# Whole-row modulation products in the opening, a longer landing time in the planner, and the spatial-gate constants in another buffer

## The chip, the cores and the metric

The kernel runs on one core of a Trainium2 chip. TensorE (PE) multiplies matrices, VectorE (DVE), ScalarE (ACT) and GpSimd (POOL) work element by element, and SyncE (SP) issues the DMAs, all of them through one queue in order. Each engine works through its own list of instructions in order, and waits at an instruction until the data and the buffers that it needs are there. The metric is the device time of one execution in microseconds; lower is better.

## The reference

Two layers of a trunk with three branches each (grouped attention, gated linear attention "GLA", and a spatial-gating unit "SGU"), over 512 latent and 256 context tokens with 1024 channels, all in float32. Cut to what matters:

```python
shift, scale, gate = split(silu(c) @ w_ada + b_ada, 3)          # 1024 x 3072
h = x * (1 + scale) + shift                                     # and hc from ctx with c_ctx
a_q, a_k, ..., s_u, s_v, s_g, m_a, m_g, m_s = split(h @ w_in)   # 1024 x 7456
y_attn = attention(a_q, a_k, a_v) * silu(a_g)
y_gla = gla(g_q, g_k, g_v, ...) * silu(g_g)
mixed = w_s @ layer_norm(s_v, ln_g, ln_b) + b_s                 # per group and 128-token chunk
y_sgu = s_u * mixed * silu(s_g)
m = sigmoid(m_a) * (y_attn @ w_br_attn) + sigmoid(m_g) * (y_gla @ w_br_gla) + sigmoid(m_s) * (y_sgu @ w_br_sgu)
x = layer_norm(alpha * x + gate * (m @ w_out), post_g, post_b)
```

## The kernel before

Every large product is made of three matmuls of split operands: a float32 array is split into a rounded high part (ACT, `hi`, `hlh`, `wh`, `yh`) and the rest (DVE, `lo`, `hll`, `wl`, `yl`; line 575, shown as L128), and high x high, high x low and low x high are summed in PSUM (`mm3`, line 625). Weights come in pieces of 256 channels x 256 columns (`raw`, three buffers).

*The planner.* Nothing runs in the order in which it is written. Each instruction is recorded, and `Sched.order` (line 138) plays the whole program through with a cost for each instruction and a latency between engines, takes the ready instruction of the best priority on each engine, and does this in 16 rounds with new priorities; the best round's order is what each engine gets (line 387). A DMA is reckoned in line 325: at the earliest 1300 ns after its issue, its bytes at 335 per ns, and then 700 ns until it has landed (line 328). That reckoned landing does not delay anything on the chip; it decides where in its engine's list an instruction that uses the data is put.

*The opening* (`start0`, line 1457). The first layer's shift and scale are dot products of rows of `w_ada` with silu(c) and silu(c_ctx). For each of eight channel blocks kb, `load` (line 1477) brings 128 rows of 1024 for the shift and 128 for the scale, and `dots` (line 1491) multiplies them with the broadcast row `srow` on DVE, in halves of 512 with a sum each: four instructions for c (v = 0, out to `junk`) and four for c_ctx (v = 1, in place in `wada`), then two small additions into `svec`. Then ACT applies `svec` to the inputs `xs`, both halves of the split are made (`hlh`/`hll` for the latent, `hch`/`hcl` for the context tokens), and PE adds this block's part of the first projection (`mmt`, line 1467). The blocks kb = 0, 1, 4 and 5 have one tile of 2 x 1024 each (tags T4 and T5), the others four tiles of 512.

*The second layer's middle.* `sgc` (line 1226) holds the four constants of the SGU: two layer-norm rows, the bias and the 128 x 512 weights. It lies in the single buffer T3, in which before it lies `yat`, the attention output, and after it `mac0`, the sum over the branches. `kept` tiles (tag S3, eight buffers) are gate values that were put to DRAM earlier and are read back: those of `sud` and `sgd` are multiplied onto the SGU's `ymix` (lines 1245 to 1249), those of `md` get a sigmoid (line 1265) and are multiplied with the first branch's products into `mac` (line 1280, `branch`). In the same stretch the dot products of the later gates run on DVE (`ada_dot`, line 676).

Of the kernel before, what the change touches and what calls it, by code (L numbers as in the profile page):

```python
# [13 lines left out]
ALU = mybir.AluOpType  # L14
# [8 lines left out]
C_GQ, C_GK, C_GV, C_GG = 1280, 1536, 1792, 2336  # L23
C_SU, C_SV, C_SG = 2848, 3360, 3872
C_MA, C_MG, C_MS = 4384, 5408, 6432


class Sched:
# [109 lines left out]
    def order(self, prio):  # L138
# [31 lines left out]
        dma, cur, ticks, acted = 0.0, None, {}, 0.0  # L170
# [10 lines left out]
        def freed(x, e):  # L181
            return x[0] + (self.lag(gone[x[1]], e) if x[1] >= 0 else 0.0)
# [33 lines left out]
        while done < n:  # L216
            best = None
            for e in engs:
# [7 lines left out]
                t = free[e] if R else (L[0][0] if L else None)  # L226
# [7 lines left out]
            t, e = best  # L234
# [25 lines left out]
            elif e in held and R and held[other[e]] > t + 1.0:  # L260

                w = held[other[e]] - t
# [25 lines left out]
            w = max((freed(x, e) for k_, c in need.items() for x in heapq.nsmallest(c, tagat[k_])), default=0.0)  # L288
# [36 lines left out]
            if e == "SP":  # L325
                dma = max(dma, st + 1300.0) + cost
                free[e] = max(st + 60.0, dma - self.AHEAD)
                end = dma + 700.0
            else:
                end = free[e] = st + cost  # L330
                if e == "ACT":
                    acted = end
                if e in held and e in self.port[i]:
                    held[e] = end
# [170 lines left out]
def kernel(ctx: ExitStack, tc: tile.TileContext, A, out, dbg=None):  # L505
    nc = tc.nc
    sc = Sched(nc)
    ACT, DVE, POOL, PE, SP = sc.ACT, sc.DVE, sc.POOL, sc.PE, sc.SP
# [8 lines left out]
    def T(tag, shape, dt=F32, name=None):  # L517
        return sc.tile(sb, shape, dt, tag, BUFS.get(tag, 1), name or tag, "SB")

    def PS(tag, shape, dt=F32):  # L520
        return sc.tile(psp, shape, dt, tag, 2, tag, "PS")
# [4 lines left out]
    def C(shape, dt=F32, name=None):  # L526
        return sc.tile(const, shape, dt, "c_" + name, 1, name, "SB")
# [5 lines left out]
    def act(out, in_, func=AF.Copy, **kw):  # L533
        return ACT.activation(out=out, in_=in_, func=func, **kw)

    def tt(eng, out, in0, in1, op):
        return eng.tensor_tensor(out=out, in0=in0, in1=in1, op=op)
# [24 lines left out]
    bcols = [pk[:, 0:24], pk[:, 24:48]]  # L562
# [10 lines left out]
    def split(hi, lo, src):  # L573
        act(hi, src)
        tta(lo, src, f(hi), ALU.subtract)
# [49 lines left out]
    def mm3(ps, L, R, first, last):  # L625

        PE.matmul(ps, L[0], R[0], start=first, stop=False)
        PE.matmul(ps, L[0], R[1], start=False, stop=False)
        PE.matmul(ps, L[1], R[0], start=False, stop=last)
# [72 lines left out]
    svecs = [C([128, 2, 8, 2], F32, name=f"svec{l}") for l in range(2)]  # L702
# [8 lines left out]
    def layer(l, X, start=None):  # L711
        full = l == 0
# [325 lines left out]
        for pr in range(2):  # L1038
# [49 lines left out]
            for gi in range(2):  # L1088
# [4 lines left out]
                for lvs in LEVELS:  # L1093
                    ps = PS("s", [128, 2, 512])
                    calls, kq, views, off, cost = [], [], {}, 0, SWITCH_PE
                    for lv in lvs:
# [23 lines left out]
                        w = 64 if lv in (1, 7) else 32  # L1120
# [21 lines left out]
                    for lv in lvs:  # L1142
                        v = views[lv]
# [69 lines left out]
        sv = T("T5", [128, 6, 512], name="sv")  # L1213
# [9 lines left out]

        lab(f"{l}sgu")

        sgc = T("T3", [128, 4, 512], name="sgc")
        lg, lb, bs, wsT = (sgc[:, i] for i in range(4))
        SP.dma_start(out=lg, in_=A["sgu_ln_g"][l].partition_broadcast(128))
        SP.dma_start(out=lb, in_=A["sgu_ln_b"][l].partition_broadcast(128))
# [56 lines left out]
        srow = ada_rows(nv)  # L1286
# [170 lines left out]
    def start0():  # L1457
        srow = ada_rows(2, "p")
        sA, sB, sC = PS("s", [128, 1024]), PS("s", [128, 1024]), PS("pt", [128, 512])
        acc = {2: (sA[:, 0:512], sA[:, 512:768]), 3: (sB[:, 0:512], sB[:, 512:768]),  # L1460
               4: (PS("p", [128, 512]), sA[:, 768:1024]), 5: (PS("p", [128, 512]), sB[:, 768:1024]),
               0: (PS("pt", [128, 512]), sC[:, 0:256]), 1: (None, sC[:, 256:512])}
        Wh = [T(t_, [128, 4, 768], F32R, name="wh") for t_ in ("T0", "T1")]
        Wl = [T(t_, [128, 4, 768], F32R, name="wl") for t_ in ("T2", "T3")]
        W = [(Wh[k // 4][:, k % 4], Wl[k // 4][:, k % 4]) for k in range(8)]

        def mmt(t, k, o, ps, joint=False):

            seg, off = ("c", t * 128) if t < 2 else ("l", (t - 2) * 128)
            H = (X0[seg][0][:, k, off:off + 128], X0[seg][1][:, k, off:off + 128])  # L1470
            n = ps.shape[-1]
            mm3(ps, H, (W[k][0][:, o:o + n], W[k][1][:, o:o + n]), k == 0 and not joint, k == 7 and not joint)

        junk = T("Q2", [128, 512], name="junk")
        part = {}

        def load(kb):
            tags = ("T4", "T5", ("hi", "hi", "lo", "lo"), ("hi", "hi", "lo", "lo"))[kb % 4]
            if kb % 4 < 2:
                t = T(tags, [128, 2, 1024], name="wada")  # L1480
                w = [t[:, j // 2, 512 * (j % 2):512 * (j % 2) + 512] for j in range(4)]
                for j in range(2):
                    SP.dma_start(out=t[:, j], in_=A["w_adaT"][0, 8 * j + kb])
            else:
                w = []
                for j in range(4):
                    w.append(T(tags[j], [128, 512], name="wada"))
                    SP.dma_start(out=w[j], in_=A["w_adaT"][0, 8 * (j // 2) + kb, :, 512 * (j % 2):512 * (j % 2) + 512])
            part[kb] = w, T("aa", [128, 2, 2, 2])

        def dots(kb, v, npool):

            w, ac = part[kb]
            for j in (0, 2, 1, 3):
                row = srow[:, v, 512 * (j % 2):512 * (j % 2) + 512]
                a = ac[:, v, j // 2, j % 2:j % 2 + 1]
                if npool == 1 and j == 3 or npool == 2 and j > 1 or npool == 3 and j:
                    o = w[j] if v else T("Q2", [128, 512], name="prod")
                    tt(POOL, o, w[j], row, ALU.mult)
                    act(o, o, accum_out=a)  # L1500
                else:
                    DVE.scalar_tensor_tensor(out=w[j] if v else junk, in0=w[j], scalar=1.0, in1=row,
                                             op0=ALU.mult, op1=ALU.mult, accum_out=a)
            if kb == 0 and v == 0:
                for b_ in bcols:
                    ts(DVE, b_[:, 8:16], b_[:, 8:16], 1.0, ALU.add)
            sv = svecs[0][:, :, kb, v]
            tt(DVE, sv, ac[:, v, :, 0], ac[:, v, :, 1], ALU.add)
            tt(DVE, sv, sv, bcols[0][:, kb:16:8], ALU.add)

        def modulate(seg, si, kb, v):
            sh, scl = (svecs[0][:, w, kb, si:si + 1] for w in range(2))
            sc.alt((ACT, "activation", dict(out=v, in_=v, func=AF.Identity, scale=scl, bias=sh)),
                   (DVE, "tensor_scalar", dict(out=v, in0=v, scalar1=scl, scalar2=sh, op0=ALU.mult, op1=ALU.add)))
            split(X0[seg][0][:, kb], X0[seg][1][:, kb], v)

        zero = T("Q2", [128, 128], F32R, name="zero")
        ts(DVE, zero, ident, 0.0, ALU.mult)

        def bank(first):  # L1520
            for s in (sA[:, 512:1024], sB[:, 512:1024], sC):
                PE.matmul(s, zero, identr.unsqueeze(1).to_broadcast([128, 4, 128]), start=first, stop=not first)

        bank(True)
        for kb in range(AH):
            load(kb)
            dots(kb, 0, NP0)
        for kb in range(8):
            if kb + AH < 8:
                load(kb + AH)  # L1530
                dots(kb + AH, 0, 0)
            xs = T("F3", [128, NT], name="xs")
            SP.dma_start(out=xs[:, sl("l")], in_=A["xT"][:, kb])
            SP.dma_start(out=xs[:, sl("c")], in_=A["ctxT"][:, kb])
            raw = T("S3", [128, 768], name="raw0")
            SP.dma_start(out=raw, in_=A["w_in"][0, kb * 128:kb * 128 + 128, 0:768])
            split(W[kb][0], W[kb][1], raw)
            modulate("l", 0, kb, xs[:, sl("l")])
            dots(kb, 1, NPOOL[kb % 2])
            modulate("c", 1, kb, xs[:, sl("c")])  # L1540
            for t in (2, 3, 4, 5, 0, 1):
                if acc[t][0] is not None:
                    mmt(t, kb, 0, acc[t][0])
                mmt(t, kb, 512, acc[t][1], True)
        bank(False)
        sc.floor = len(sc.ops)

        def st_b(q, ev_kv):
            for t in (2, 3, 4, 5, 0, 1):
                if acc[t][0] is not None:  # L1550
                    act(q[:, t], acc[t][0].rearrange("p (h d) -> p h d", h=8))
                ev_kv(acc[t][1], t)
            ps = PS("p", [128, 512])
            for k in range(8):
                mmt(1, k, 0, ps)
            act(q[:, 1], ps.rearrange("p (h d) -> p h d", h=8))

        return st_b
# [78 lines left out]
```

## Time and profile before

| | us |
|---|---|
| median of 3 runs (lowest, highest) | 1430.35 (1429.0, 1435.49) |
| profiled execution, its own time | 1431.16 |
| its span in the trace | 1429.3 |
| PE busy in the span | 1387.9 |
| DVE, ACT, POOL busy | 1032.5, 671.3, 164.5 |

The profiled execution took 1.86 us more than its span. PE is busy for 97% of it, so what can be lost or won on the chain that ends last is mostly PE's idle time (about 41 us), and the time in which PE works at a lower clock. A row of the trace gives the start and the duration in us, the engine and the line of the recording helper (L421 or L128 for nearly all), the operation with output <- inputs by their program names, and in square brackets how long the engine sat idle before it and what ended that.

### The profile page before, as it was taken

What the parts mean: (1) busy time and instruction counts of PE and PEld (TensorE: products, weight loads), DVE (VectorE), ACT (ScalarE), POOL (GpSimd) and SP (SyncE); (2) the same over time, 40 slices, a digit from 0 to 9 for tenths busy, and PEclk for the clock granted to TensorE, in tenths of its full rate; (3) what the DMA queues carried; (4) which work ended last, traced back from release to release, by engine and by line L of the source; (5) the groups of instructions that cost most, each with busy time, mean ns of one, the idle gap of its engine ahead of it and who ended that gap; (6) DMA issues with size and microseconds to landing.
All of it is one profiled execution on the core that took longest, in us unless ns stands there. A gap on an engine that the chain in (4) does not pass through costs nothing.

```text
span 1429.3 us, 27382 instructions
## 1 busy us (share of the span) xinstructions
PE 1387.9 (97%) x10724; PEld 1227.5 (86%) x10724; DVE 1032.5 (72%) x2206; ACT 671.3 (47%) x1293; POOL 164.5 (12%) x261
## 2 busy tenths in 40 slices
PE   8999999999999999999999999999999998999997
PEld 5798899987888888888889999998987877888887
DVE  8968877897977678732147684897799876645396
ACT  4566667844464323212232174666774554422331
POOL 0021100034330000000000020110014320000003
PEclk9999999999999999999999999999999999999999
DMA  9410012332356765521224232112243467535542
GB/s 321 160 45 9 23 31 65 124 94 64 93 177 207 250 200 169 158 67 45 65 77 148 66 119 71 30 31 60 82 148 90 117 193 252 168 97 177 182 144 94
DMA packets 123956, 168.55 MB, mean 118 GB/s; under 512 B 9497, under 2 KB 90801, under 8 KB 123825
## 3 DMA queue, kind: packets, MB, share of 16 engines
q1 hardware_dynamic: 123826, 166.79, 37.4%
q8 instruction: 84, 1.38, 0.4%
q14 instruction: 46, 0.38, 0.1%
HBM read 143.41 MB, written 23.34 MB: 117 GB/s over the span
## 4 chain that ended last, share of the span: by engine, by line
PE 73%; DVE 16%; DMA 5%; issue 2%; ACT 2%; POOL 1%; SPq 0%; POOLq 0%; DVEq 0%; ACTq 0%
PE p L421 60%; PE pt L421 8%; PE s L421 4%; DVE M L128 3%; DVE lo L128 2%; DMA wada<-in_w_adaT_dram 2%; DVE wada L421 1%; DVE sm L421 1%; DVE junk L421 1%; DMA raw<-in_w_in_dram 1%; PE s L119 1%; DVE PTs L421 1%; DMA sgc<-in_sgu_b_dram 1%; DVE cs L421 1%; POOL sf L421 0%
## 5 line engine op out<-in xcount | busy, mean ns | idle before, releaser
L128 DVE TENSOR_TENSOR lo<-raw,hi 128x512 fp32r<-128x512 f32 (+1 forms) x293 | 202.4, 700 | 173.7 <-ACT hi L421 166.2
L421 ACT ACTIVATE hi<-raw 128x512 fp32r<-128x512 f32 (+1 forms) x296 | 185.8, 634 | 233.2 <-PE p L421 149.8
L421 PE MATMUL p<-hlh,hi 128*128 128x512 f32 x704 | 280.9, 399 | 2.5 <-DVE mac L421 1.5
L421 PE MATMUL p<-hlh,lo 128*128 128x512 f32 x704 | 280.7, 399 | 1.5 <-DVE lo L128 1.3
L421 PE MATMUL p<-hll,hi 128*128 128x512 f32 x704 | 278.6, 396 | 0.0
L421 PEld LDWEIGHTS p<-hlh,lo 128*128 128x128 f32 x704 | 132.4, 188 | 31.6 <-DVE lo L128 2.1
L421 PEld LDWEIGHTS p<-hlh,hi 128*128 128x128 f32 x704 | 132.3, 188 | 29.8 <-ACT hi L421 2.2
L421 PEld LDWEIGHTS p<-hll,hi 128*128 128x128 f32 x704 | 132.3, 188 | 26.5
L421 PE MATMUL p<-hch,lo 128*128 128x256 f32 x368 | 104.5, 284 | 0.0
L421 PE MATMUL p<-hch,hi 128*128 128x256 f32 x368 | 104.2, 283 | 0.0
L421 PE MATMUL p<-hcl,hi 128*128 128x256 f32 x368 | 104.0, 283 | 0.0
L421 PE MATMUL p<-hi,hlh 128*128 128x256 f32 (+1 forms) x352 | 102.0, 290 | 0.0
L421 PE MATMUL p<-hi,hll 128*128 128x256 f32 (+1 forms) x352 | 100.8, 286 | 0.0
L421 PE MATMUL p<-lo,hlh 128*128 128x256 f32 (+1 forms) x352 | 99.8, 284 | 0.0
L421 POOL TENSOR_SCALAR sf<-sf 128x1 f32<-128x1 f32 x20 | 7.5, 374 | 642.3 <-DVE sf L421 641.9
L421 PE MATMUL p<-yh,hi 128*128 128x512 f32 (+1 forms) x192 | 70.0, 364 | 7.8 <-DVE mac L421 6.7
L421 ACT ACTIVATE P<-s,sm 128x768 f32<-128x768 f32 (+1 forms) x80 | 65.4, 821 | 23.5 <-DVE sm L421 23.2
L421 DVE TENSOR_REDUCE sm<-s 128x1 f32<-128x768 f32 (+1 forms) x72 | 65.0, 921 | 12.4 <-PE s L421 12.2
L421 DVE TENSOR_TENSOR PTs<-pt,PTs 128x512 fp32r<-128x512 f32 x104 | 69.2, 685 | 4.1 <-ACT PTs L421 3.1
L421 PEld LDWEIGHTS p<-hcl,hi 128*128 128x128 f32 x368 | 69.3, 188 | 2.1
L421 PEld LDWEIGHTS p<-hch,hi 128*128 128x128 f32 x368 | 69.5, 189 | 1.9
L421 DVE SCALAR_TENSOR_TENSOR wada<-wada,srow 128x512 f32<-128x512 f32 x96 | 65.1, 687 | 8.0 <-DMA wada<-in_w_adaT_dram 6.7
(299 smaller groups left out, 3352.1 us busy)
## 6 DMA issues: line engine op xcount, KB each, us to landing
raw<-in_w_in_dram SPq DMA_DIRECT2D x204, 256.0 KB, 3.0
wada<-in_w_adaT_dram SPq DMA_DIRECT2D x80, 256.0 KB, 4.9
raw<-in_w_out_dram SPq DMA_DIRECT2D x32, 256.0 KB, 2.9
raw<-in_w_in_dram SPq DMA_DIRECT2D x16, 272.0 KB, 3.1
wada<-in_w_adaT_dram SPq DMA_DIRECT2D x8, 512.0 KB, 4.9
raw<-in_w_br_attn_dram SPq DMA_DIRECT2D x16, 256.0 KB, 3.4
raw<-in_w_br_gla_dram SPq DMA_DIRECT2D x16, 256.0 KB, 3.0
raw<-in_w_br_sgu_dram SPq DMA_DIRECT2D x16, 256.0 KB, 3.3
```

The costliest lines, as they stand in the source:

```text
L119: return self.record(eng.n, lambda: [getattr(eng.e, m)(*a, **k) for m, a, k in calls], outs, ins, cost, None, dens)
L128: fns[p.n] = lambda real=real, k=k: real(**k)
L421: return s.record(n, lambda: real(*a, **k), outs, ins, _cost(n, meth, outs, ins, k), _table(n, k), _dens(n, ins, k), _port(n, meth, outs, ...
```

## The change

Three things are changed. The 700 ns of reckoned landing become 2000. In the second layer (`full` is false there) `sgc` takes a buffer of the tag `hc`, in which the context half of the split input lies until its last projection. And for the blocks kb = 1, 4 and 5 the tile has a third row of 1024, and `dots` multiplies whole rows: two instructions of 1024 per v with one sum each, out to the third row for v = 0, and one small addition instead of two.

```diff
+LAND = 2000.0
...
                 dma = max(dma, st + 1300.0) + cost
                 free[e] = max(st + 60.0, dma - self.AHEAD)
-                end = dma + 700.0
+                end = dma + LAND
...
-        sgc = T("T3", [128, 4, 512], name="sgc")
+        sgc = T("T3" if full else "hc", [128, 4, 512], name="sgc")
...
-                t = T(tags, [128, 2, 1024], name="wada")
-                w = [t[:, j // 2, 512 * (j % 2):512 * (j % 2) + 512] for j in range(4)]
+                t = T(tags, [128, 3, 1024], name="wada")
+                w = [t[:, 0], t[:, 1], t[:, 2]] if kb else [t[:, j // 2, 512 * (j % 2):512 * (j % 2) + 512] for j in range(4)]
...
             w, ac = part[kb]
+            sv = svecs[0][:, :, kb, v]
+            if kb % 4 < 2 and kb:
+                for j in range(2):
+                    DVE.scalar_tensor_tensor(out=w[j] if v else w[2], in0=w[j], scalar=1.0, in1=srow[:, v],
+                                             op0=ALU.mult, op1=ALU.mult, accum_out=ac[:, v, j, 0:1])
+                tt(DVE, sv, ac[:, v, :, 0], bcols[0][:, kb:16:8], ALU.add)
+                return
```

Since the planner reckons with other landings and costs, it puts out another order on every engine. DVE in the opening, before, from the split of block 4's latent part (`hll`) to the low part of block 5's weights (`wl_93<-raw0_135`):

```order
L128 TENSOR_TENSOR hll_76<-xs_127,hlh_75 128x512
L421 TENSOR_TENSOR svec0_73<-svec0_73,pk_70 128x2
L421 SCALAR_TENSOR_TENSOR junk_94,aa_126<-wada_122,srow_79 128x512
L128 TENSOR_TENSOR hcl_78<-xs_120,hch_77 128x256
L421 SCALAR_TENSOR_TENSOR wada_114,aa_115<-wada_114,srow_79 128x512
L421 SCALAR_TENSOR_TENSOR junk_94,aa_126<-wada_124,srow_79 128x512
L421 SCALAR_TENSOR_TENSOR wada_114,aa_115<-wada_114,srow_79 128x512 x3
L421 SCALAR_TENSOR_TENSOR junk_94,aa_126<-wada_123,srow_79 128x512
L421 SCALAR_TENSOR_TENSOR junk_94,aa_126<-wada_125,srow_79 128x512
L421 TENSOR_TENSOR svec0_73<-aa_115 128x2
L128 TENSOR_TENSOR wl_93<-raw0_135,wh_91 128x768
```

Four of the eight products here are block 4's second set (`wada_114`), the other four block 6's first. The same place in the changed kernel, between the same two splits:

```order
L131 TENSOR_TENSOR hll_76<-xs_127,hlh_75 128x512
L424 TENSOR_TENSOR svec0_73<-aa_111 128x2
L424 SCALAR_TENSOR_TENSOR wada_118,aa_119<-wada_118,srow_79 128x1024
L424 TENSOR_TENSOR svec0_73<-svec0_73,pk_70 128x2
L424 SCALAR_TENSOR_TENSOR wada_114,aa_115<-wada_114,srow_79 128x1024
L424 TENSOR_TENSOR svec0_73<-aa_119,pk_70 128x2
L131 TENSOR_TENSOR wl_93<-raw0_135,wh_91 128x768
```

Between the two splits stood eight products of 512, and now two of 1024. Counted over the whole opening, 56 products of 512 stood ahead of the split `hll` of the seventh block, and now 30 of 512 and 12 of 1024; ahead of the eighth block's 60, and now 35 and 12. All 64 products were of 512 before; 40 are now, and 12 are of 1024.

SP's queue in the second layer, before, from the second store of the gate values `md_0` to the first read of the last `sud` values; `sgc` stands far behind the attention:

```order
L421 DMA md_0_1806<-keep 128x512
L421 DMA sgc<-in_sgu_ln_g_dram 128x512
L421 DMA sgc<-in_sgu_ln_b_dram 128x512
L421 DMA sgc<-in_sgu_wT_dram 128x512
L421 DMA sgc<-in_sgu_b_dram 128x512
L421 DMA raw<-in_w_in_dram 128x2x256
L421 DMA kept<-sud_1740 128x512
```

In the changed kernel `sgc` follows on the ten weight pieces of the projections in which the context half is used for the last time:

```order
L424 DMA raw<-in_w_in_dram 128x2x256 x10
L424 DMA sgc<-in_sgu_ln_g_dram 128x512
L424 DMA sgc<-in_sgu_ln_b_dram 128x512
L424 DMA sgc<-in_sgu_wT_dram 128x512
L424 DMA raw<-in_w_in_dram 128x2x256
L424 DMA sgc<-in_sgu_b_dram 128x512
L424 DMA pgx<-in_post_g_dram 128x1024
```

That is ahead of all stores of gate values, more than fifty rows of SP's list earlier. The first `md` value is read back behind the last of the `sgd` values and two loads of `wada` in both; all `md` values were stored by then, and now only the first is.

DVE in the second layer, before, from the last SGU products to the first two products into `mac`:

```order
L421 TENSOR_TENSOR ymix<-pt,sgc 128x4x128 x3
L128 TENSOR_TENSOR ymix<-ymix,kept 128x512 x4
L128 TENSOR_TENSOR lo<-raw,hi 128x512
L128 TENSOR_TENSOR ymix<-ymix,kept 128x512
L128 TENSOR_TENSOR lo<-raw,hi 128x512
L128 TENSOR_TENSOR ymix<-ymix,kept 128x512 x3
L421 SCALAR_TENSOR_TENSOR wada,gs<-wada,srow 128x512
L421 TENSOR_TENSOR mac_2215<-p,kept 128x512 x2
```

In the changed kernel, from the last product onto `ymix` to the first into `mac`:

```order
L131 TENSOR_TENSOR ymix<-ymix,kept 128x512
L424 SCALAR_TENSOR_TENSOR wada,gs<-wada,srow 128x512 x2
L131 TENSOR_TENSOR lo<-raw,hi 128x512 x3
L424 SCALAR_TENSOR_TENSOR wada,gs<-wada,srow 128x512 x2
L131 TENSOR_TENSOR lo<-raw,hi 128x512 x4
L424 SCALAR_TENSOR_TENSOR wada,gs<-wada,srow 128x512 x2
L131 TENSOR_TENSOR lo<-raw,hi 128x512
L424 TENSOR_TENSOR mac_2215<-p,kept 128x512
```

Between the SGU's last product and the first into `mac` stood one other instruction, and now fourteen. On PE, the SGU's last matmuls (`pt<-sgc,sv`) stood behind the first eight matmuls of the branch; now they stand about 120 matmuls of 512 columns ahead of it. All eight products `sv<-sv,sgc` stood behind the GLA on DVE, and stand now inside it.

## Rows read from the trace of the kernel before

**Rows 1.** The page: busy time of each engine with its share and count, and the chain that ended last, by engine.

```profile
PE 1387.9 (97%) x10724; PEld 1227.5 (86%) x10724; DVE 1032.5 (72%) x2206; ACT 671.3 (47%) x1293; POOL 164.5 (12%) x261
...
PE 73%; DVE 16%; DMA 5%; issue 2%; ACT 2%; POOL 1%; SPq 0%; POOLq 0%; DVEq 0%; ACTq 0%
```

**Rows 2.** PE's waits over the whole execution: what it waited for, us in total, times, longest.

```profile
PE p L421 <- DVE mac L421: 8.2, 4, 5.2
PE s L119 <- DVE M L128: 3.6, 5, 1.4
PE s L421 <- DVE wl L128: 3.5, 3, 1.3
```

**Rows 3.** PE in order of time, in the opening: the first product and those before which it sat idle.

```profile
13.09 1.22 PE L421 MATMUL s<-wh,hlh 128*128 128x512 f32 x2 [2.54 <-ACT hlh L421]
...
34.35 0.73 PE L421 MATMUL s<-wl,hlh 128*128 128x512 f32 x2 [1.13 <-DVE wl L128]
...
41.39 0.73 PE L421 MATMUL s<-wl,hlh 128*128 128x512 f32 x2 [1.16 <-DVE wl L128]
...
48.51 0.74 PE L421 MATMUL s<-wl,hlh 128*128 128x512 f32 x2 [1.26 <-DVE wl L128]
...
56.22 0.50 PE L421 MATMUL s<-wh,hll 128*128 128x512 f32 x1 [0.70 <-DVE hll L128]
```

**Rows 4.** DVE in order of time, in the opening: a wait for a load, and the seventh block.

```profile
9.59 0.69 DVE L421 SCALAR_TENSOR_TENSOR junk<-wada,srow 128x512 f32<-128x512 f32 x1 [0.35 <-DMA wada<-in_w_adaT_dram]
...
53.32 0.95 DVE L128 TENSOR_TENSOR wl<-raw,wh 128x768 fp32r<-128x768 f32 x1
54.19 0.68 DVE L421 SCALAR_TENSOR_TENSOR wada<-wada,srow 128x512 f32<-128x512 f32 x1
...
54.80 0.68 DVE L421 SCALAR_TENSOR_TENSOR wada<-wada,srow 128x512 f32<-128x512 f32 x1
...
55.41 0.15 DVE L421 TENSOR_TENSOR svec<-aa 128x2 f32<-128x2 f32 x1
55.49 0.68 DVE L128 TENSOR_TENSOR hll<-xs,hlh 128x512 fp32r<-128x512 f32 x1
56.09 0.15 DVE L421 TENSOR_TENSOR svec<-svec,pk 128x2 f32<-128x2 f32 x1
```

**Rows 5.** Busy time in a stretch of 10 us of the opening: after the stretch and its length, busy us (count) of PE, PE's weight loads, DVE, ACT, POOL, then the granted clock, the DMA share and GB/s.

```profile
10.00:20.00 10.00, 7.46 (x25) 5.72 (x24) 9.90 (x33) 5.34 (x8) 0.00 (x0) 1.00 1.04 397
```

**Rows 6.** PE in order of time around its longest wait.

```profile
1211.93 0.80 PE L421 MATMUL p<-yh,hi 128*128 128x512 f32 x1 [5.21 <-DVE mac L421]
...
1215.93 0.63 PE L421 MATMUL p<-yh,hi 128*128 128x512 f32 x1
1216.36 0.51 PE L421 MATMUL p<-yl,hi 128*128 128x512 f32 x1
1216.71 0.40 PE L421 MATMUL p<-yh,lo 128*128 128x512 f32 x1
1216.94 0.40 PE L421 MATMUL p<-yh,hi 128*128 128x512 f32 x1
```

**Rows 7.** A stretch, as in rows 5, right behind that wait (granted clock: third figure from the end).

```profile
1212.00:1213.00 1.00, 1.00 (x3) 0.82 (x4) 1.00 (x3) 0.00 (x0) 0.00 (x0) 0.50 0.97 334
```

**Rows 8.** DVE, SP and ACT in order of time on the way to that wait.

```profile
1176.44 0.69 DVE L128 TENSOR_TENSOR yl<-yat,yh 128x512 fp32r<-128x512 f32 x1
...
1177.62 0.38 SPq L421 DMA_DIRECT2D sgc<-in_sgu_ln_g_dram  x1
...
1182.12 2.02 DVE L128 TENSOR_TENSOR sv<-sv,sgc 128x512 f32<-128x512 f32 x3 [2.25 <-DMA sgc<-in_sgu_ln_g_dram]
...
1203.78 2.50 DVE L128 TENSOR_TENSOR ymix<-ymix,kept 128x512 f32<-128x512 f32 x4
...
1205.70 0.93 SPq L421 DMA_DIRECT2D kept<-md  x2
...
1209.23 1.28 ACT L421 ACT_TABLE_LOAD   x1 [2.02 <-DMA kept<-md]
...
1210.52 1.15 ACT L421 ACTIVATE kept<-kept 128x512 f32<-128x512 f32 x2
...
1211.18 1.29 DVE L421 TENSOR_TENSOR mac<-p,kept 128x512 f32<-128x512 f32 x2 [0.69 <-ACT kept L421]
```

**Rows 9.** The first layer's first branch: DVE's waits for loads, and PE's behind them.

```profile
513.67 0.69 DVE L421 SCALAR_TENSOR_TENSOR prod<-wada,srow 128x512 f32<-128x512 f32 x1 [3.10 <-DMA wada<-in_w_adaT_dram]
...
515.76 0.50 PE L421 MATMUL p<-yh,hi 128*128 128x512 f32 x1 [1.50 <-DVE mac L421]
...
534.02 0.47 PE L421 MATMUL p<-hlh,hi 128*128 128x512 f32 x1 [0.76 <-DVE mac L421]
...
560.23 0.50 PE L421 MATMUL p<-hlh,hi 128*128 128x512 f32 x1 [0.73 <-DVE mac L421]
```

**Rows 10.** The page: DMA issues, KB each, median us from issue to landing.

```profile
raw<-in_w_in_dram SPq DMA_DIRECT2D x204, 256.0 KB, 3.0
...
wada<-in_w_adaT_dram SPq DMA_DIRECT2D x80, 256.0 KB, 4.9
```

**Rows 11.** The second layer's GLA: a stretch as in rows 5; and from the first layer's GLA, PE's longest wait for it.

```profile
1040.00:1060.00 20.00, 19.78 (x106) 16.40 (x105) 19.40 (x37) 15.88 (x28) 0.05 (x1) 1.00 0.58 171
...
345.19 0.71 PE L119 MATMUL s<-M 64*32 64x64 f32 x48 [1.42 <-DVE M L128]
```

## The prediction

> **What bounds the kernel now.** I read the page's busy times and chain first: PE is busy for 1387.9 of 1429.3 us and holds 73% of the chain that ended last [rows 1]. So a change counts only where PE waits, or works slowly because it has waited. PE's own waits, the second view, name three places where this happens for long: a product whose PSUM buffer DVE has to empty into `mac` (8.2 us in four waits, the longest 5.2), the level products of the GLA, which wait for `M` (3.6), and the opening, which waits for the low parts of the weights, `wl` (3.5) [rows 2]. The third view is PE in order of time at these places. In the opening PE waits 1.13, 1.16, 1.26 and 0.70 us, 4.25 together, and each time for DVE [rows 3]; DVE is busy for 9.90 of 10 us there [rows 5], and the seven microseconds from one block to the next are its own. The longest wait, 5.21 us, stands in the second layer at the first branch product [rows 6].
>
> **The whole rows in the opening.** One product of 512 and its sum take 0.61 us from start to start (54.19 to 54.80) [rows 4]. No row shows one of 1024. What the length costs is read from the two plain splits: 0.87 us for 768 columns (53.32 to 54.19), 0.60 for 512 (55.49 to 56.09), so 0.27 for 256 and 0.54 for 512 more. A whole row is then an estimated 0.61 + 0.54 = 1.15 us against 1.22 for two halves, 0.07 less. Its bounds are 0.87, the row of 768, and 1.22, no gain; I take 1.15, since both splits lie on that line. Twelve pairs are merged: 12 x 0.07 = 0.84 us. Six additions fall away, each 0.08 (55.41 to 55.49) [rows 4]: 0.48.
>
> The Trainium skill's page "VectorE: DVE Perf Modes", section "The TRN2 errata — SBUF-src ops pay a fixed extra latency per instruction", gives a fixed term of about 150 cycles to each such instruction, 0.16 us at 0.96 GHz, paid once by a large tile and by each of many small ones. By that the twelve pairs would give an estimated 1.9 us instead of 0.84; the start-to-start times here do not agree, since the next product begins before that term is over.
>
> The order brings more than the merging. Ahead of the seventh block's `hll` stood 56 products of 512, and stand now 30 and 12 whole rows, worth 54; ahead of the eighth's 60, and now worth 59. Two products put off are 1.22 us, one is 0.61. The wait of 0.35 us for a load at 9.59 [rows 4] goes too, because the first block's second set now stands between. Seventh block: 0.84 + 1.22 + 0.48 + 0.35 = 2.9 us earlier; eighth: 0.84 + 0.61 + 0.48 + 0.35 = 2.3. What is late next is the eighth block, so I take 2.4 us. Above, it ends at the 4.25 us that PE waits at all; from then on PE is the bound. Below, the loads: the DMA engines are busy to 1.04 of their time at 397 GB/s [rows 5]. If they cannot bring blocks faster, DVE's gain turns into waits for `wada` and nothing is won, or 0.4 lost, one such wait more. The two products that are put off lie later beside PE's backlog: PE waits for nothing between 56.22 and the end of the opening.
>
> **The constants' buffer.** The way to the long wait is one chain [rows 8]. `yat` is split until 1177.1; only then is T3 free and `sgc` issued, at 1177.62; DVE stands 2.25 us for it until 1182.12; the SGU's products follow, are ready at 1203, and are multiplied with the `kept` values until 1206; this frees the S3 buffers into which `md` is read, from 1205.70 on; ACT waits for that until 1209.23, loads the sigmoid's table for 1.28 us, and DVE empties the first product into `mac` at 1211.18. PE has filled its two PSUM buffers by then and stands still for 5.21 us [rows 6]. Behind the wait the granted clock is 0.50, the lower of the two levels [rows 7]: products of 512 start 0.43 us apart (1215.93 to 1216.36) instead of 0.23 (1216.71 to 1216.94) [rows 6]. From 1211.93 to 1216.36 ten of them take 4.43 us where ten at full clock take 2.3: another 2.1 us. With `sgc` in `hc` the first link is gone: it is issued right behind the last context projection, the SGU's products run inside the GLA, and its last matmuls stand 120 products, 120 x 0.23 = 28 us, ahead of the branch. `md` is then read back long before its product, and the sigmoid's table load with it. I take the whole 5.21 + 2.1 = 7.3 us. The bounds: 7.3, and nothing, if another wait stands in the same place.
>
> What is moved costs DVE time inside the GLA: eight products `sv<-sv,sgc` at 0.60, 4.8 us, where DVE is busy for 19.40 of 20 us [rows 11]. It is hidden by PE's projections for later stages, of which 28 us are still left behind the GLA; PE would have to wait for `M` as in the first layer (1.42 us in one wait [rows 11]) for it to count. Bounds 0 and 4.8; I take 0. `sgc` and `pgx` wait on SP's queue for the last context projection, with weight pieces queued behind them; `pgx` stood there before, so this costs nothing new.
>
> **The longer landing.** A weight piece of 256 KB was reckoned at 1.3 + 0.78 + 0.7 = 2.8 us from issue to landing and is now at 4.1. It takes 3.0 in the median, a `wada` piece of the same size 4.9 [rows 10]. So the old figure was right for quiet stretches and short by 2 us for crowded ones. This is what the first layer's first branch shows: DVE stands 3.10 us at a product whose `wada` has not landed, with the next `mac` behind it, and PE waits 1.50 us; in the same manner 0.76 and 0.73, 2.99 in all [rows 9]. With 4.1 the planner puts such products later; still short of 4.9. I take a third of the 2.99, 1.0 us, with bounds 0 and 2.99. Everywhere else the new order is another throw: apart from the places above, PE's waits behind the opening sum up to some 14 us in about twenty pieces, the largest 1.42 [rows 11]. I take 0 for the difference and 3 us either way.
>
> **The sum.** 2.4 + 7.3 + 1.0 = 10.7 us off the profiled execution's own 1431.16 gives 1420.5; that execution is 0.8 above the median of the runs, and I forecast **1420** for the median.
>
> **The rivals.**
>
> *Another wait takes the place of the long one.* For it speaks that the branch begins in a crowd of loads, `wada` pieces and `md` reads, and that in-order DVE has stood behind `wada` for up to 3.1 us [rows 9]; in the new order six `wada` products stand ahead of the first `mac`. Against it, eight weight splits stand between them too. PE would wait 1.5 to 3 us there, and up to 2 at the next product: 1420 + 3 to 5 = 1423 to 1425, I say 1424. Chance 0.18.
>
> *The longer landing gains nothing, and the opening is bound by its loads.* Then 7.3 us or a little more is left: 1431.2 - 7.3 = 1423.9, less 0.8 to the median, 1423. Chance 0.12. The Trainium skill's page "DMA: Bandwidth & Descriptors", section "Anatomy of one DMA — SWDGE (gpsimd) path", speaks for it: a fit of about 2.0 us and the bytes over 436 KB per us, by which 256 KB land after an estimated 2.6 us and the old figure was long enough; the 4.9 us of `wada` do not agree, as they hold the queue ahead.
>
> *Slower.* The SGU's products inside the GLA decide it: once DVE's 4.8 us there are no longer covered, PE waits in the level products as in the first layer, 1.4 us at a time, and one wait as long as the 5.21 us brings the low clock with its 2.1 as well. It decides from the point at which PE's projections run out before the GLA ends. With a new wait at the branch as well (the 7.3 stay) and nothing from the landing: 1430.4 - 2.4 + 4.8 + 2.1 = 1435; with 3 us of bad throw 1438. Against it: 28 us of projections stand behind the GLA. Chance 0.08.
>
> *More of it.* All waits for loads go and the opening becomes PE's: 4.25 + 7.3 + 2.99 + some 2 of smaller ones = 16.5, so 1414. Chance 0.15.
>
> **How the numbers follow.** The forecast, 1417 to 1423.5, has 0.47. The range is 1412 to 1429: it takes in all but the slower case and the far ends. Within 0.5%, about what a measurement of this kernel tells from no change, is 1423.2 to 1437.5. Faster: the forecast's 0.47 nearly whole, the 0.15, and some of the first two rivals, 0.65; slower 0.06; the rest 0.29.
>
> **What would show it.** Right: no PE wait over 2 us around the first branch of the second layer, and a granted clock of 1.00 there; `sgc` of the second layer issued before 1080; whole rows 1.15 us from start to start, and PE's four waits in the opening down to some 2 us. Wrong: DVE in the opening idle for `wada`; PE waiting for `M` in the second GLA; or a new wait at a `mac` behind a load. If the long wait goes and the time does not fall by 7 us, the throw of the order has taken it back, and PE's waits by place will say where.

## The result, and the profile after

The changed kernel takes 1415.6 us (median of 4 runs, 1414.14 to 1417.27) where the kernel before took 1432.71 in the runs beside it: ratio 0.9883, 95% interval 0.9853 to 0.9912. Forecast were 1420 and a range of 1412 to 1429. The four runs of the kernel before lie at 1429.0, 1430.35, 1435.08 and 1435.49; beside the experiments below, in 13 to 18 runs each on three chips, its median is 1430.25 to 1430.82. So of the 17 us some 15 can be relied on, against a forecast of 10.7, and the terms have to be gone through one by one. The profiled execution took 1415.44 (span 1413.7, 15.6 less than before).

The page of the changed kernel, busy times and chain (answers to [rows 1]):

```profile
PE 1386.2 (98%) x10724; PEld 1227.2 (87%) x10724; DVE 1037.7 (73%) x2199; ACT 677.7 (48%) x1298; POOL 149.3 (11%) x237
...
PE 79%; DVE 14%; ACT 3%; issue 3%; POOL 1%; DMA 0%; POOLq 0%; SPq 0%; DVEq 0%; ACTq 0%
```

PE does the same 10724 matmuls in 1.7 us less busy time, and its idle time falls from 41.4 to 27.5 us. The DMAs, 5% of the chain before, are gone from it. PE's waits, us in total, times, longest (answers to [rows 2]):

```profile
PE pt L424 <- DVE PTs L424: 3.5, 6, 0.9
PE s L122 <- DVE M L131: 2.4, 2, 1.5
PE s L424 <- ACT hlh L424: 2.3, 5, 0.7
PE s L122 <- issue: 2.1, 1, 2.1
```

No wait for `mac` is left (8.2 us before), and none for `wl` (3.5). Where the 15.6 us arise is read from when the same instruction starts in both traces:

| PE or DVE reaches | before | after | lead of after |
|---|---|---|---|
| last `pt<-wh,hcl` of the opening | 68.4 | 66.4 | 2.0 |
| first branch product of layer 1 | 505.6 | 502.4 | 3.2 |
| first `mac<-mac,sgS` of layer 1 | 734.4 | 725.0 | 9.4 |
| first `p<-hi,mlh` of layer 1 | 763.7 | 754.8 | 8.9 |
| last `mac<-p,kept` of layer 2 | 1225.8 | 1208.0 | 17.8 |
| last `p<-hi,mlh` | 1420.6 | 1404.2 | 16.4 |

*The opening.* PE in order of time (answers to [rows 3]), the first product and the three longest waits behind it:

```profile
11.23 1.22 PE L424 MATMUL s<-wh,hlh 128*128 128x512 f32 x2 [0.68 <-ACT hlh L424]
24.74 0.73 PE L424 MATMUL s<-wh,hlh 128*128 128x512 f32 x2 [0.43 <-ACT hlh L424]
50.24 0.73 PE L424 MATMUL s<-wh,hlh 128*128 128x512 f32 x2 [0.62 <-ACT hlh L424]
52.85 0.50 PE L424 MATMUL s<-wh,hll 128*128 128x512 f32 x1 [0.48 <-DVE hll L131]
```

DVE in order of time (answers to [rows 4]): a whole row, and `hll` of the seventh and the eighth block.

```profile
20.31 1.22 DVE L424 SCALAR_TENSOR_TENSOR wada<-wada,srow 128x1024 f32<-128x1024 f32 x1
21.45 0.08 DVE L424 DVE_READ_ACCUMULATOR wada<-wada,srow 128x1 f32 x1
...
52.11 0.68 DVE L131 TENSOR_TENSOR hll<-xs,hlh 128x512 fp32r<-128x512 f32 x1
...
57.77 0.68 DVE L131 TENSOR_TENSOR hll<-xs,hlh 128x512 fp32r<-128x512 f32 x1
```

The whole row takes 1.14 us from start to start (the reading of its sum, at 21.45, begins together with the next instruction). `hll` comes 3.4 us earlier in the seventh block (55.49 before) and 2.5 in the eighth (60.28).

*The second layer.* SP, PE and DVE in order of time (answers to [rows 6, 8]): the constants, the SGU's last matmuls, the first read of `md`, the first product into `mac`.

```profile
983.96 0.34 SPq L424 DMA_DIRECT2D sgc<-in_sgu_ln_g_dram  x1
...
1161.98 1.05 PE L424 MATMUL pt<-sgc,sv 128*128 128x128 f32 x8
...
1169.67 0.38 SPq L424 DMA_DIRECT2D kept<-md  x1
...
1191.15 0.39 PE L424 MATMUL p<-yh,hi 128*128 128x512 f32 x1
...
1194.13 0.69 DVE L424 TENSOR_TENSOR mac<-p,kept 128x512 f32<-128x512 f32 x1 [0.79 <-PE p L424]
```

The SGU's last matmuls stand 28 us ahead of the branch (1163 to 1191), `md` is read 21 us ahead of it, and DVE now waits for PE. The granted clock (third figure from the end) stays at 1.00 in the branch, where it was 0.50 [rows 7]; the second stretch is one of the GLA, in which PE's busy share has not fallen [rows 11]:

```profile
1195.00:1196.00 1.00, 1.00 (x6) 0.80 (x5) 0.05 (x1) 0.63 (x1) 0.00 (x0) 1.00 0.89 293
...
1040.00:1060.00 20.00, 19.88 (x197) 15.80 (x196) 19.19 (x53) 11.51 (x26) 3.13 (x8) 1.00 0.39 110
```

### The profile page after: what moved, and what is told of

It reads as the page before. It is cut to its first block, busy times and chain, and to the rows that moved or that the text cites. A ratio compares the mean times of both kernels' runs of the same rounds, so it can differ in the third digit from the quotient of the medians.

```text
span 1413.7 us, 27304 instructions
## 1 busy us (share of the span) xinstructions
PE 1386.2 (98%) x10724; PEld 1227.2 (87%) x10724; DVE 1037.7 (73%) x2199; ACT 677.7 (48%) x1298; POOL 149.3 (11%) x237
## 4 chain that ended last, share of the span: by engine, by line
PE 79%; DVE 14%; ACT 3%; issue 3%; POOL 1%; DMA 0%; POOLq 0%; SPq 0%; DVEq 0%; ACTq 0%
PE p L424 66%; PE pt L424 7%; PE s L424 4%; DVE M L131 2%; DVE lo L131 1%; DVE sm L424 1%; DVE wada L424 1%; PE s L122 1%; DVE PTs L424 1%; DVE St L424 1%; DVE P L131 1%; DVE qx L131 1%; DVE junk L424 1%; ACT L424 1%; ACT ez L424 1%
## 5 line engine op out<-in xcount | busy, mean ns | idle before, releaser
L424 DVE SCALAR_TENSOR_TENSOR wada<-wada,srow 128x512 f32<-128x512 f32 (+1 forms) x96 | 71.2, 754 | 4.4 <-DMA wada<-in_w_adaT_dram 3.0
L424 PEld LDWEIGHTS p<-hch,lo 128*128 128x128 f32 x368 | 69.2, 188 | 0.2
```

The lines of the kernel that those rows point to most:

```text
L424: return s.record(n, lambda: real(*a, **k), outs, ins, _cost(n, meth, outs, ins, k), _table(n, k), _dens(n, ins, k), _port(n, meth, outs, ...
```

## The experiments

Twelve kernels were run: each edit alone, each left out, other landings, and another buffer for `md`. One table first, since it carries the main reading. *Last SGU matmul* is the end of the last `pt<-sgc,sv` of the second layer, *md read* the issue of the first `kept<-md` there, both in us from the branch's first product (negative: ahead of it); *wait* is PE's longest at a product into `mac` in that branch; *layer 1* is what PE waits for DVE at `mac` and at `sig` (a gate that is computed in the branch itself) in the first layer's branches, summed. The kernel before stands with its profiled execution and with the median that stands ahead of the prediction; ratios are to the runs of before on the same chip.

| kernel | landing | last SGU matmul | md read | wait | layer 1 | median | ratio (95%) |
|---|---|---|---|---|---|---|---|
| before | 700 | +4.8 | +7.5 | 5.21 | 3.98 | 1430.35 | |
| constants alone | 700 | +6.6 | +10.5 | 7.80 | 2.81 | 1438.87 | 1.0039–1.0068 |
| rows alone | 700 | +4.8 | +7.5 | 5.32 | 1.75 | 1425.56 | 0.9943–0.9975 |
| all but landing | 700 | +7.7 | +10.7 | 8.18 | 0.79 | 1432.42 | 0.9997–1.0023 |
| landing alone | 2000 | +2.3 | +5.7 | 4.45 | 0.37 | 1426.89 | 0.9953–0.9978 |
| all but constants | 2000 | +2.3 | +5.0 | 4.54 | 0 | 1424.47 | 0.9945–0.9971 |
| all but rows | 2000 | −28.2 | −21.7 | 0 | 0.67 | 1417.53 | 0.9881–0.9913 |
| changed kernel | 2000 | −28.1 | −21.5 | 0 | 0 | 1415.6 | 0.9853–0.9912 |
| changed, 1300 | 1300 | +4.8 | +7.5 | 5.37 | 0 | 1426.68 | 0.9953–0.9980 |
| changed, 1900 | 1900 | +4.8 | +7.5 | 5.46 | 0 | 1423.18 | 0.9941–0.9968 |
| changed, 2100 | 2100 | +0.2 | +3.4 | 4.05 | 0 | 1424.97 | 0.9939–0.9966 |
| changed, 2100, md in F3 | 2100 | +0.2 | −0.9 | 0.17 | 0 | 1414.62 | 0.9876–0.9902 |
| all but constants, md in F3 | 2000 | +2.3 | −1.3 | 0 | 0 | 1417.39 | 0.9896–0.9922 |
| all but landing, md in F3 | 700 | +3.2 | −9.8 | 0.61 | 0.58 | 1423.91 | 0.9943–0.9972 |

**The constants alone.**

```diff
-        sgc = T("T3", [128, 4, 512], name="sgc")
+        sgc = T("T3" if full else "hc", [128, 4, 512], name="sgc")
```

> Kernel before with one edit: the second layer's gate constants in the buffer of the context half; landing and opening as before. Theory (terms add): the 5.21 us wait at the first branch product of the second layer and the 2.1 us of low clock behind it go, 1432.7 - 7.3 = 1425.4, and the opening and the first layer stay as they were. Rival 'another wait in the same place': a wait of 1.5 to 5 us is left at a product into mac in the second layer, time 1428 to 1433. Rival 'throw of the order': the time falls anywhere between 1422 and 1433 while waits of the first layer, which the edit does not touch, change by more than 1 us.

Slower by half a per cent, outside what the theory and both rivals gave. The trace, SP, PE and DVE in order of time at the branch:

```profile
1193.72 1.84 SPq L421 DMA_DIRECT2D kept<-agd  x4
...
1197.99 1.12 PE L421 MATMUL pt<-ident,o 128*128 128x128 f32 x4 [3.58 <-DVE o L421]
...
1211.36 0.33 SPq L421 DMA_DIRECT2D kept<-md  x1
...
1217.80 0.69 DVE L421 TENSOR_TENSOR mac<-p,kept 128x512 f32<-128x512 f32 x1 [1.36 <-ACT kept L421]
1218.55 0.79 PE L421 MATMUL p<-yh,hi 128*128 128x512 f32 x1 [7.80 <-DVE mac L421]
```

`sgc` is issued by 983 and the products `sv<-sv,sgc` are done in the GLA, as the prediction had it, but the matmuls `pt<-sgc,sv` still stand in the branch. T3 need no longer be freed for the constants, and in the planner's order the attention's values `agd` are now read at 1193.72 instead of 1161; `yat`, `oT` and `ymix` are all gated in the branch itself, and `md`, last in line, is read later than before. The rival of another wait in the same place describes it, at a higher price than it named: the wait is 2.6 us longer than before, and PE waits 3.58 us for `o`, the GLA's output, where it waited 0.45.

**The landing alone.**

```diff
-                end = dma + 700.0
+                end = dma + 2000.0
```

> Kernel before with one edit: 2000 in place of 700 ns of reckoned landing. Theory: the 5.21 us wait stays, because its chain starts with T3 being free at 1177 and not with a late load; gone are waits behind late loads in the first layer's first branch (2.99 us and what follows them), so 1427 to 1431. Rival 'landing is enough': the long wait goes too, PE waits nowhere over 2 us, 1420 to 1424. Rival 'landing gains nothing': 1432 to 1434.

1426.89, 0.1 under the theory's range: the long wait stays, the first layer's are nearly gone. PE's rows at both places:

```profile
554.70 0.50 PE L421 MATMUL p<-hlh,hi 128*128 128x512 f32 x1 [0.37 <-DVE mac L421]
...
1206.55 0.73 PE L421 MATMUL p<-yh,hi 128*128 128x512 f32 x1 [4.45 <-DVE mac L421]
```

**The rows alone** (the diff's last two pieces; landing 700, constants in T3).

> Kernel before with one edit: whole rows of 1024 in blocks 1, 4 and 5 of the opening; landing 700 and constants in T3 as before. Theory: the eighth block's hll is done 2.3 to 2.5 us earlier and the rest follows, 1430.3. Rival 'opening bound by its loads': DVE idle for wada, the eighth block under 1 us earlier, 1432 to 1433. Rival 'throw of the order': the opening gains its 2.4 but later waits differ by more than 2 us either way.

1425.56. The opening ends at 67.3 against 68.4, the eighth `hll` stands at 58.9 against 60.3: 1.1 to 1.4 us, less than forecast. The other 4 us of the gain do not come from the rows as such, since they arise in later stretches that the edit does not touch; the largest seen is 2.2 us less waiting in the first layer's branches. By the rival's description that is a throw of the order; no run separates it further.

**Each edit left out.** The changed kernel with one edit undone:

```diff
-        sgc = T("T3" if full else "hc", [128, 4, 512], name="sgc")
+        sgc = T("T3", [128, 4, 512], name="sgc")
```

> Changed kernel with the constants put back into T3; whole rows and landing of 2000 stay. Theory (terms add): the long wait and the low clock behind it come back, 1415.6 + 7.3 = 1422.9. Rival 'the longer landing alone would have removed the wait': no PE wait over 3 us in the second layer's first branch, 1415 to 1418.

```diff
-LAND = 2000.0
+LAND = 700.0
```

> Changed kernel with 700 ns of reckoned landing again; whole rows and constants in hc stay. Terms add (what each edit did alone: rows 0.9959, constants 1.0053): 1432 x 0.9959 x 1.0053 = 1434. Theory 'the constants' move needs the longer landing': as with the constants alone, reads of the gate values agd are issued only at about 1190, the SGU's last matmuls stand in the branch, and PE waits over 5 us at a product into mac in the second layer; 1430 to 1436. Rival 'the slower time with the constants alone was an accident of that one order': the wait is under 3 us, 1417 to 1424.

> Changed kernel with halves of 512 again in blocks 1, 4 and 5; constants in hc and landing of 2000 stay. Theory: no PE wait over 3 us in the second layer, as in the changed kernel, and only the opening is longer, by 2.2 us at the eighth block's hll (60.0 against 57.8, as the kernel with the longer landing alone has it) and 2 us at the end: 1417.5 to 1418.5. Rival 'throw of the order': the opening loses 2.2, but later waits differ by more than 2 us either way.

All three came as the theory had it: 1424.47 (1.6 above the figure), 1432.42 and 1417.53. Without the longer landing `agd` is read at 1186.88 and PE waits longer than before at both places:

```profile
1191.15 1.11 PE L424 MATMUL pt<-ident,o 128*128 128x128 f32 x4 [3.58 <-DVE o L424]
...
1211.61 0.80 PE L424 MATMUL p<-yh,hi 128*128 128x512 f32 x1 [8.18 <-DVE mac L424]
```

So the edits do not add: the constants cost 8 us by the landing of 700 (6.9 beside the rows, 1432.42 − 1425.56), and bring 8.9 (1424.47 − 1415.6) by 2000. Without the rows (the diff's last two pieces undone) it is the opening that is longer: the eighth `hll` at 60.0 against 57.8, its end at 68.2 against 66.4, the time 1.9 more.

**Other landings** (the changed kernel, with 2100, 1300 and 1900).

```diff
-LAND = 2000.0
+LAND = 2100.0
```

> Changed kernel with 2100 ns in place of 2000. It asks how much a nearly empty change of the planner's numbers moves the time. Theory 'the landing's size matters, not the throw': 1413 to 1418, no PE wait over 3 us in the second layer. Rival 'throw of the order': a time over 1419 or under 1412, or a wait over 3 us at a product into mac.

> Changed kernel with 1300 ns, nearly half of the step from 700 to 2000. Theory 'dose': the 256 KB pieces are reckoned at 3.4 us, still short of the 4.9 that wada takes, so a part of the waits at mac is left, 1417 to 1428. Rival 'threshold in the order of the gate reads': agd read early as with 2000 and time 1414 to 1418, or late as with 700 and 1428 or more.

> Changed kernel with 1900 ns in place of 2000. Theory 'the planner's order decides by where it puts the last SGU matmul': with this matmul over 15 us ahead of the branch's first product there is no wait over 2 us at a product into mac and the time is 1413 to 1419; with it under 5 us ahead there is a wait of 4 to 8 us and the time is 1422 to 1428. Rival 'nearer to the landing that the loads take, the shorter': 1900 lies between 1300 and 2000, and the time between 1426.7 and 1415.6 near the latter, 1416 to 1418, wherever that matmul stands.

At 2100, 100 ns more, the kernel is 9 us slower; PE in order of time:

```profile
1164.55 0.38 PE L424 MATMUL pt<-sgc,sv 128*128 128x128 f32 x2
...
1193.21 1.50 PE L424 MATMUL pt<-sgc,sv 128*128 128x128 f32 x12
...
1204.31 0.50 PE L424 MATMUL p<-yh,hi 128*128 128x512 f32 x1 [4.05 <-DVE mac L424]
```

Most of the SGU's matmuls are where the changed kernel has them, but the last twelve stand at 1193; `ymix` waits for them, its products hold the S3 buffers, and `md` is read only at 1197.87. At 1900 and at 1300 all 32 of these matmuls stand at the branch (from 1187 and from 1191 on), and PE waits 5.46 and 5.37 us; 1423.18 is what the theory of the last SGU matmul gave for that place, and 1426.68 lies in the range of 'dose', but the wait is whole and not a part. Both "the size of the landing decides" and "nearer to the real landing is better" fall: of five values run with all three edits (700 among them), one puts that matmul early.

**Another buffer for `md`.** What the nine kernels with a long wait share is that `md` is read behind the branch's first product. SP's own waits in the kernel before, from 1200 to 1206.5, name what its queue stands for there (us in total, times, longest):

```profile
SPq L421 <- DVE ymix L128: 3.7, 4, 3.2
```

These four waits stand before two pieces of `wada`, which lie in S3 too, and the first two of `md`. If the S3 buffer is the last link, it must be enough to take `md` out of S3, into F3, a pool of three other buffers:

```diff
-                        sg = T("S3", [128, NQ], name="kept")
+                        sg = T("S3" if full else "F3", [128, NQ], name="kept")
```

> Whole rows and landing of 2000, constants in T3 as in the kernel before, and md read into F3 tiles. Theory 'the last link is the S3 buffer': the waits of 4.54 and 0.47 us go without moving the constants, and the low clock with them: 1424.5 - 5 - 2 = 1417.5, 1416 to 1420. Rival 'constants late in T3 keep DVE behind': the last SGU products on DVE still stand ahead of the first product into mac and PE waits 2 to 5 us for it, 1421 to 1425.

> Changed kernel with 2100 in place of 2000 and md read into F3 tiles. Theory 'the last link is the S3 buffer': the wait of 4.05 us and the low clock behind it go, 1425 - 4.5 - 2 = 1418.5, 1416 to 1420. Rival 'the 9 us between 2000 and 2100 lie in many small waits': the long wait goes and the time stays over 1421.

> Whole rows and constants in hc, landing of 700, and one edit more: the second layer's md values are read into tiles of the tag F3 and no longer of S3, so that they need not wait for the SGU's ymix products to free S3 buffers. Theory 'the last link is the S3 buffer': md is issued before the ymix products, and PE's 8.18 us wait at a product into mac falls below 2, with the low clock behind it: 1432.4 - 8 - 2 = 1422, 1420 to 1425. Rival 'PE and DVE are late there for the attention's values agd, and md is not the last link': a wait over 4 us stays, 1428 to 1434.

The constants are in T3 in the first of these, as before, and the last SGU matmul still comes 2.3 us behind the branch's first product. All but the constants, with `md` in S3, then in F3; SP, ACT, DVE and PE in order of time:

```profile
1195.58 1.41 SPq L424 DMA_DIRECT2D kept<-md  x2
...
1200.07 1.28 ACT L424 ACT_TABLE_LOAD   x1 [1.40 <-DMA kept<-md]
...
1202.03 1.29 DVE L424 TENSOR_TENSOR mac<-p,kept 128x512 f32<-128x512 f32 x2 [1.03 <-ACT kept L424]
1202.77 0.79 PE L424 MATMUL p<-yh,hi 128*128 128x512 f32 x1 [4.54 <-DVE mac L424]
```

```profile
1190.28 0.93 SPq L424 DMA_DIRECT2D kept<-md  x2
...
1193.69 1.28 ACT L424 ACT_TABLE_LOAD   x1 [2.46 <-DMA kept<-md]
...
1197.05 0.68 DVE L424 TENSOR_TENSOR mac<-p,kept 128x512 f32<-128x512 f32 x1
```

The stretch from 1200 to 1210 in the same two kernels (columns as in [rows 5]):

```profile
1200.00:1210.00 10.00, 7.22 (x24) 5.48 (x24) 4.53 (x12) 3.73 (x6) 0.00 (x0) 0.83 0.81 263
```

```profile
1200.00:1210.00 10.00, 10.00 (x45) 8.13 (x44) 8.26 (x18) 4.30 (x7) 0.00 (x0) 1.00 0.85 274
```

`md` is read 5.3 us earlier, in front of the `ymix` products instead of among them, the wait is gone and the clock stays at 1.00: 1424.47 becomes 1417.39. These 7.1 us are 5.01 of waiting (4.54 and 0.47) and 2.1 that is left for the low clock and all else; a granted clock of 0.83 over 10 us accounts for at most 1.7 of them. At 2100 the same edit brings 10.3 us, of which 4.5 are those waits; PE's waits between 62 and 470, which the edit does not touch, fall by 3.3 as well, and it is busy for 3.9 us less. Without the longer landing it brings 8.5. The rival of late attention values falls there: `agd` is read at 1194.11, as late as with the constants alone, but behind `md`, and the wait is 0.61; a wait of 3.58 for `o` stays (the profiled execution, 1429.75, is the longest of ten of this kernel). In all three kernels with `md` in F3 PE waits at most 0.61 us there, whatever stands in T3 and whatever landing is reckoned. All three times bear out the theory rather than its rivals; the one at 2100 came 1.4 us under its range and is level with the changed kernel.

## Why the prediction was right, and where its reasons were not

**The opening: right.** 2.4 us were forecast, 2.0 is the lead at its end, and leaving the rows out costs 1.9; the rows alone, with the old landing, lead by 1.1 there. The pair's pace was 1.14 us (estimated 1.15 against 1.22), so the page "VectorE: DVE Perf Modes" of the Trainium skill, section "The TRN2 errata — SBUF-src ops pay a fixed extra latency per instruction", is not borne out start to start: 0.08 us are saved by a pair, half of the estimated 0.16 that its fixed term of 150 cycles would save. The eighth block was put at 2.3 earlier and came 2.5. Not foreseen: the first block's first set of products now ends first, so that PE starts at 11.23 instead of 13.09; the longer landing alone does that too (11.7 for the first `hll` against 13.8). The fear that the loads bind did not come true: DVE is busy for 10.00 of 10 us from 10 to 20.

**The longer landing: mis-sized.** 1.0 of 2.99 was taken; all of it went, and a fourth wait of 0.99 for `sig`. PE over the first layer's branches, in both kernels:

```profile
505.60:734.40 228.80, 224.54 (x1275) 195.14 (x1274) 113.60 (x270) 59.97 (x109) 0.00 (x0) 1.00 0.37 112
```

```profile
502.40:725.00 222.60, 222.60 (x1271) 194.42 (x1270) 117.99 (x280) 61.31 (x111) 0.00 (x0) 1.00 0.40 118
```

4.26 us of idle time became none, and the stretch 6.2 shorter; the rest is busy time, with four matmuls fewer in it. The step that failed was "still short of 4.9": DVE still stands for `wada`, but where no full PSUM buffer is queued behind; in order of time:

```profile
498.19 0.69 DVE L424 SCALAR_TENSOR_TENSOR prod<-wada,srow 128x512 f32<-128x512 f32 x1 [3.13 <-DMA wada<-in_w_adaT_dram]
...
534.89 0.69 DVE L424 SCALAR_TENSOR_TENSOR prod<-wada,srow 128x512 f32<-128x512 f32 x1 [2.02 <-DMA wada<-in_w_adaT_dram]
```

With 700 the five kernels wait 0.58 to 3.98 us here and the stretch takes 224.4 to 228.9 us, with 1300 or more the nine wait 0 to 0.67 and it takes 222.6 to 223.6: so the landing shortens it. But not all of the 6.2 us are its own, since the other edits, which do not touch the stretch, take up to 4.5 of them at 700, and all but the landing is only 1.8 us longer here than the changed kernel. The rival of the loads quotes, from the page "DMA: Bandwidth & Descriptors" of the Trainium skill, section "Anatomy of one DMA — SWDGE (gpsimd) path", a fit for DMAs that GpSimd issues. The loads here are SP's: 256 KB of weights take 3.0 us in the median [rows 10] where the fit gives an estimated 2.6. The median landing of `wada` fell from 4.9 [rows 10] to 4.3 us on the way.

**The constants' buffer: the size right, the cause wrong.** 7.3 us, 5.21 of waiting and 2.1 of low clock, is about what such a wait is worth: taking one of 4.54 and 0.47 us away by itself gave 7.1. But the step "with `sgc` in `hc` the first link is gone ... `md` is then read back long before its product" does not follow. The chain [rows 8] was read from its beginning, and its end decides: `md` needs S3 buffers that are held until the `ymix` products are done. With early constants the planner is free to put the SGU's last matmuls early, and did so in two of the seven orders run with `md` in S3, both with 2000. In the other five the rival of another wait was right, with 4.05 to 8.18 us. The placing was read off the changed order, and by it the wait had to go; what was wrong was to give the edit the credit. That 2000 is the one landing of the five whose order does this is luck of the change: with 1900 or 2100 the long wait would have stayed.

Nothing was paid in the GLA, as forecast: PE's waits between 890 and 1180 are 4.0 us, 5.5 before.

**The throw: too small.** ±3 us were allowed. 100 ns more or less of landing move the time by 9.4 and 7.6. Of the 17.8 us of lead at the last `mac`, 2.0 are the opening's, 1.2 come in the first layer's attention and GLA, 6.2 in its branches, 0.5 are lost behind them, and 8.9 are the long wait with small ones around it; the end gives 2.2 back, 0.7 of it in two waits at 1364 and 1385, the rest was not traced. By the profiled executions, 15.7 us, the result lies between the forecast's 10.7 us and the 16.5 of the rival "more of it", and in part for the reason that this one gave at the loads.

## What to carry to other kernels

Read a chain of waits from its end: the last link, here a pool of buffers handed out in program order, is what has to be cut, and cutting it held in all three orders tried, while removing the first link took the wait away in two of seven. Where a planner sets the order, a result of one setting says little about the edit: run the neighbours (here 100 ns to either side cost 8 to 9 us) before giving an edit the credit. An optimistic load time costs where a full PSUM buffer is queued behind the instruction that waits.

## What was not expected of the hardware

The spread of the runs goes with the reckoned landing. The five kernels with 700 differ by 5.3 to 8.8 us from run to run (before: 1427.52 to 1434.89 in 18 runs), the nine with more by 0.5 to 4.3 (6 to 18 runs each against 4 to 8). It may be that their orders lean on loads that land late in some executions; that was not tested.

After one wait the low clock came late. With the landing of 2100 PE waited 4.05 us until 1204.31; the granted clock is 1.00 in the first of these stretches, then 0.79, 0.50 and 0.86:

```profile
1202.00:1204.00 2.00, 0.00 (x0) 0.00 (x0) 1.85 (x6) 1.97 (x3) 0.00 (x0) 1.00 0.94 264
1204.00:1206.00 2.00, 1.69 (x6) 1.38 (x7) 0.85 (x2) 0.00 (x0) 0.00 (x0) 0.79 0.82 221
1206.00:1208.00 2.00, 2.00 (x6) 1.54 (x5) 0.42 (x1) 0.00 (x0) 0.00 (x0) 0.50 0.92 314
1208.00:1210.00 2.00, 2.00 (x9) 1.61 (x8) 0.92 (x4) 0.00 (x0) 0.00 (x0) 0.86 1.01 378
```

This wait of 4 us is thus paid for after it has ended. And in the changed kernel PE sits idle for 2.06 us at 406.98, amid 96 small matmuls, with nothing that the profile names as the releaser; in none of the other thirteen kernels does such a wait reach 0.6 us. What held it stays open.
